# Moving the causal mask of the SSD branch from the exponent to the score block, and the log decays from GpSimd to VectorE

## The chip, the core and the metric

The kernel runs on one core of a Trainium2 chip. The metric is device time in microseconds (us), the median of several executions; lower is better. TensorE (PE) does the matrix products, VectorE (DVE), ScalarE (ACT) and GpSimd (POOL) the elementwise work, each from a queue of its own in program order. SyncE (SP) issues the weight loads; ACT issues some DMAs from its own queue.

## The reference

One decoder layer over 256 tokens of width 2048. A combined projection feeds stick-breaking attention, a Mamba-2 SSD branch and memory cross-attention; each branch is projected back, weighted by sigmoid gates and summed, and an output projection, a residual and a final norm follow. The part that the change touches is the SSD scan, 32 heads of 64 channels in 8 groups:

```python
a_cum = jnp.cumsum(a_dt, axis=-1)                       # dt * a, never positive
tri = jnp.tril(jnp.ones((l, l), dtype=bool))
seg = a_cum[..., :, None] - a_cum[..., None, :]
decay_in = jnp.exp(jnp.where(tri, seg, -jnp.inf))       # 0 for sources later than the target
cb = jnp.einsum('bclgn,bcsgn->bcgls', cm, bm)           # scores, one block per group
y_diag = jnp.einsum('bcgls,bgecls,bcsgep->bclgep', cb, decay_in, xs)
```

A head's weight from source token s to target token t is thus the score times exp of the difference of two running sums where s <= t, and 0 elsewhere.

## The kernel before

**Weight products.** Nearly all time goes to products of the 256 tokens with weight matrices. `gemm` makes 512 columns at a time. It walks the contraction in chunks of two tiles of 128: SP loads a chunk of 512 KB (`raw`), ACT rounds it to a high part (`wh`, L139), DVE forms the remainder (`wl`, L143), and PE does twelve products of 512 columns (L230 high x high, L231 with `wl`, L232). `wh` and `wl` have three buffers each, so that PE reads one chunk while the next two are made: ACT can begin chunk n when PE has left chunk n - 3.

**Order by hand.** The instructions of each engine run as they are traced. After each chunk `pump` traces what was put off until now (`defer`) and one step of one of two lanes of background work, in turn; a lane so advances every second chunk. A step is what a generator does up to its next `yield`.

**The background work around the change.** `ssd_group(g)` is one group of four heads; groups 0, 2, 4, 6 stand in one lane, 1, 3, 5, 7 in the other. It runs beside the gate products and the projections of the memory and stick-breaking branches: four pairs of eight and four chunks for either branch, 96 chunks in all. The lanes get their first SSD step at the eighth of them. Before the third branch the lanes are emptied (`finish()`). The steps of a group:

1. PE transposes the group's x (`xp`, L656). ACT issues two DMAs that spread rows of `acT`, the running sums by head, over all partitions: two tiles `dec`, each of two heads by two halves of the tokens, 128x512 (L661).
2. ACT copies `xp` to `xn` (L666). POOL adds the mask `dmask` (0 or -1e30) to each `dec` (L674) and then the source's running sum `nac`, once for each half (L677): six instructions. Behind them POOL makes `xs`, `xn` and `xe` (L681 to L684), five instructions. PE makes the scores `cb` (L687, L688).
3. ACT copies the score block between the halves (L690) and takes Exp of both `dec` (L692).
4. DVE multiplies both `dec` by `cb`, which it reads from PSUM (L695).
5. PE applies them to `xs` (`y`, L702) and makes `off` (L704).
6. to 8. DVE adds the parts and gates them (L706 to L711), ACT and POOL make the group norm (L714, L132, L133), and ACT scales (L719).

`ssd_cols` afterwards turns the eight results round (`dot`, L732), two steps for each group.

Of the kernel before, what the change touches and what calls it, by code (L numbers as in the profile page):

```python
# [16 lines left out]
P = 128  # L17
D = 2048          # model width
T = 256           # tokens, and memory tokens
NKT = D // P  # L20
GW = 512          # columns of a weight group
KC = 2            # k-tiles per weight chunk
# [18 lines left out]
def trunk_kernel(  # L41
# [35 lines left out]
    def tq(shape, n):  # L77
        return tmp.tile(shape, F32, tag="tq", name=nm(n), bufs=2)
# [3 lines left out]

    def bank(shape, n="bank"):
        return psB.tile(shape, F32, tag="bank", name=nm(n))
# [15 lines left out]
    # keeps the array busy, so that its clock is up when the first operands arrive  # L100
# [8 lines left out]
    tri = const.tile([P, P], F32, name="tri")          # [s, t] = 1 where s <= t  # L109
    nc.gpsimd.affine_select(out=tri, in_=ones, compare_op=ALU.is_ge, fill=0.0,  # L110
                            base=0, pattern=[[1, P]], channel_multiplier=-1)
    smask = const.tile([P, P], F32, name="smask")      # 0 where k < q, else NEG
    dmask = const.tile([P, P], F32, name="dmask")      # 0 where s <= t, else NEG
    nc.gpsimd.memset(dmask, 0.0)
    for m, op in ((smask, ALU.is_gt), (dmask, ALU.is_ge)):
        nc.gpsimd.affine_select(out=m, in_=dmask, compare_op=op, fill=NEG, base=0,
                                pattern=[[1, P]], channel_multiplier=-1)
# [17 lines left out]
    def split(*parts):  # L135
        """hi + lo = src * scale for each (hi, lo, src, scale), hi and lo in the form of
        float32r."""
        for hi, _, src, scale in parts:
            nc.scalar.activation(hi, src, AF.Copy, **({} if scale is None else {"scale": scale}))  # L139
        for hi, lo, src, scale in parts:  # L140
            h32 = hi.bitcast(F32)
            if scale is None:
                nc.vector.tensor_tensor(lo, src, h32, ALU.subtract)  # L143
            else:
                nc.vector.scalar_tensor_tensor(lo, src, scale, h32, ALU.mult, ALU.subtract)

    class Cols:
        """A [K, 256] operand by k-tiles, in slots of 8 k-tiles, as hi and lo."""
# [12 lines left out]
    def defer(fn, chunks=LATE):  # L161
        """Has fn traced that many weight chunks later."""
        cnt[0] += 1
        heapq.heappush(late, (now[0] + chunks, cnt[0], fn))
# [9 lines left out]
    def pump():  # L174
        """Once per weight chunk: what was put off until now, and one step of a lane of the
        work that runs beside the weight products."""
        now[0] += 1
        while late and late[0][0] <= now[0]:
            heapq.heappop(late)[2]()
        advance(lanes[now[0] % 2])  # L180
# [19 lines left out]
    def gemm(lhs, nk, w, c0, evac, cols=False, along=None, sizes=None):  # L200
        """evac gets lhs @ w[:, c0:c0 + 512], in two banks: by halves of the tokens, or
        with cols transposed, by pairs of blocks of 128 columns."""
        acc = [psA.tile([P, GW], F32, tag="acc", name=nm("acc")) for _ in range(2)]
        k0 = 0
        for kc in sizes or [KC] * (nk // KC):
            raw = load_chunk(w, c0, GW, k0, kc)
            wh = stage.tile([P, kc, GW], F32R, tag="wh", name=nm("wh"))
            wl = stage.tile([P, kc, GW], F32R, tag="wl", name=nm("wl"))
            split((wh, wl, raw, None))
            if along is not None:  # L210
                along(k0)
            for j in range(kc):
                kt = k0 + j
                lh, ll = lhs.at(kt)
                first, last = kt == 0, kt == nk - 1
                if cols:
                    for b in range(4):
                        a = acc[b // 2][:, (b % 2) * T:(b % 2 + 1) * T]
                        bs = slice(b * P, (b + 1) * P)
                        nc.tensor.matmul(a, wh[:, j, bs], lh, start=first and b % 2 == 0,  # L220
                                         stop=False, skip_group_check=True)
                        nc.tensor.matmul(a, wh[:, j, bs], ll, start=False, stop=False,  # L222
                                         skip_group_check=True)
                        nc.tensor.matmul(a, wl[:, j, bs], lh, start=False, stop=last,  # L224
                                         skip_group_check=True)
                    continue
                for t in range(2):
                    a = acc[t]
                    tt = slice(t * P, (t + 1) * P)
                    nc.tensor.matmul(a, lh[:, tt], wh[:, j], start=first, stop=False)  # L230
                    nc.tensor.matmul(a, lh[:, tt], wl[:, j], start=False, stop=False)  # L231
                    nc.tensor.matmul(a, ll[:, tt], wh[:, j], start=False, stop=last)  # L232
            k0 += kc
            pump()
        if cols:
            acc = [a.rearrange("p (b t) -> p b t", t=T) for a in acc]
        defer(lambda: evac(acc))

    def to_cols(dst, b0, scale):
        """Evacuates a transposed group into blocks dst[:, b0 + i, token]."""  # L240
# [43 lines left out]
    def squares(raw, acc, q, first=None):  # L284
        """Adds the squares of 4 k-tiles to acc, by tokens."""
# [12 lines left out]
    def scale_steps(rs, rbc, acc):  # L298
        """1 / rms of the 256 tokens, on the tokens' own partitions and then on every one."""
# [64 lines left out]
    # the gains and the first k-tile in one  # L364
# [18 lines left out]
    acT = dram.tile([SSD_HEADS, T], F32, name="acT")  # L383

    def dt_steps():
        """The step sizes' projection, transposed: the 32 columns' high and low parts side by
        side as the stationary operand, then one sum over both."""
# [26 lines left out]
        # log1p(e) = 2 atanh(e / (2 + e)), e in [0, 1]  # L414
# [17 lines left out]
        # nac = - cumulative sum of dt * a in each half = cumulative sum of dt * exp(a_log)  # L432
# [6 lines left out]
        # decays to the end of the first half, and from there  # L439
# [104 lines left out]
    oS = Cols(8, "oS")  # L544
    ra = const.tile([P, P], F32R, name="ra")           # 1 where s > t
    rb = const.tile([P, P], F32R, name="rb")           # 1

    def sb_head(h):
        hs = slice(h * P, (h + 1) * P)
        # blocks (k, q) of 128 by 128: (0, 0), (1, 1), (0, 1)  # L550
# [22 lines left out]
        # the last block of the second product goes unused: it makes 256 columns  # L573
# [23 lines left out]
    def start_sb():  # L597
        nc.gpsimd.tensor_tensor(tri, ones, tri, ALU.subtract)     # now 1 where s > t
# [50 lines left out]
    def ssd_group(g):  # L649
# [18 lines left out]
        xe = tq([P, 3, P], "xe")       # 256 of xs at the edge, 128 of cb  # L668
# [3 lines left out]
        for i, d in enumerate(dec):  # L672
            d4 = d.rearrange("p h q t -> p (h q) t")
            nc.gpsimd.tensor_tensor(d4, d4, dmask.unsqueeze(1).to_broadcast([P, 4, P]), ALU.add)  # L674
            for q in range(2):
                h2 = slice(4 * g + 2 * i, 4 * g + 2 * i + 2)
                nc.gpsimd.tensor_tensor(d[:, :, q], d[:, :, q],  # L677
                                        nac[:, q, h2].unsqueeze(2).to_broadcast([P, 2, P]),
                                        ALU.add)
# [10 lines left out]
        nc.scalar.activation(xe[:, 2], cb[:, 1], AF.Copy)  # L690
        for d in dec:
            nc.scalar.activation(d, d, AF.Exp)  # L692
        yield
        for d in dec:
            nc.vector.tensor_tensor(d, d, cb[:, 0:3:2].unsqueeze(1).to_broadcast([P, 2, 2, P]),  # L695
                                    ALU.mult)
# [157 lines left out]
    # the last group half by half, so that one half's end hides under the other  # L854
# [30 lines left out]
def lay_out(inputs):  # L885
    """Every array without its leading 1; x, mem and the vectors by channels also or only
    channel-major, [channel % 128, channel // 128, ...]."""
# [29 lines left out]
```

## Time and profile before

| what | value |
|---|---|
| time, median of 3 executions | 1259.33 us (1258.82 to 1260.66) |
| profiled execution, span of the core | 1256.4 us |
| PE busy | 1239.0 us (99%) |
| DVE busy | 760.4 us (61%) |
| ACT busy | 596.6 us (47%) |
| POOL busy | 172.9 us (14%) |

No other time of the profiled execution is given than its span; the median stands 2.9 us above it. The profile records start and duration of each instruction. Where an engine waits, a row names the time and the instruction that ended it. Matmuls overlap: their ends are modelled, and the next one starts before the one in front has ended.

### The profile page before, as it was taken

What the parts mean: (1) busy time and instruction counts of PE and PEld (TensorE: products, weight loads), DVE (VectorE), ACT (ScalarE), POOL (GpSimd) and SP (SyncE); (2) the same over time, 40 slices, a digit from 0 to 9 for tenths busy, and PEclk for the clock granted to TensorE, in tenths of its full rate; (3) what the DMA queues carried; (4) which work ended last, traced back from release to release, by engine and by line L of the source; (5) the groups of instructions that cost most, each with busy time, mean ns of one, the idle gap of its engine ahead of it and who ended that gap; (6) DMA issues with size and microseconds to landing.
All of it is one profiled execution on the core that took longest, in us unless ns stands there. A gap on an engine that the chain in (4) does not pass through costs nothing.

```text
span 1256.4 us, 18790 instructions
## 1 busy us (share of the span) xinstructions
PE 1239.0 (99%) x7512; PEld 1109.7 (88%) x7512; DVE 760.4 (61%) x925; ACT 596.6 (47%) x734; POOL 172.9 (14%) x178
## 2 busy tenths in 40 slices
PE   9999999999999999999999999999999999999997
PEld 7899999999988889999999787877888888888886
DVE  7765554555544545788888765564665555555554
ACT  6653433443444554434554554555444444444443
POOL 3500000000000000010100616436111110110101
PEclk9999999999999999999999999999999999999999
DMA  8666566654566666565666666646566676667573
GB/s 300 223 203 176 160 188 176 183 166 142 163 194 193 184 169 185 169 179 169 172 173 199 190 184 202 209 145 193 181 179 199 201 203 199 184 193 246 198 240 120
DMA packets 124681, 236.57 MB, mean 188 GB/s; under 512 B 10128, under 2 KB 11568, under 8 KB 124464
## 3 DMA queue, kind: packets, MB, share of 16 engines
q1 hardware_dynamic: 118272, 224.01, 60.0%
q10 hardware_dynamic: 6320, 11.35, 2.7%
q8 instruction: 59, 0.97, 0.3%
q14 instruction: 30, 0.25, 0.1%
HBM read 233.20 MB, written 2.13 MB: 187 GB/s over the span
## 4 chain that ended last, share of the span: by engine, by line
PE 88%; POOL 5%; DMA 2%; DVE 2%; issue 1%; ACT 1%; POOLq 0%; SPq 0%; ACTq 0%; DVEq 0%
PE acc L231 15%; PE acc L232 15%; PE acc L230 15%; PE acc L220 12%; PE acc L222 12%; PE acc L224 12%; POOL dec L677 2%; POOL dec L674 2%; DMA raw<-in_w_mem_kv_dram 1%; PE y L702 1%; DMA dec<-acT 1%; DVE wl L143 1%; POOL xn L683 1%; PE acc L873 1%; PE acc L874 1%
## 5 line engine op out<-in xcount | busy, mean ns | idle before, releaser
L143 DVE TENSOR_TENSOR wl<-raw,wh 128x1024 fp32r<-128x1024 f32 (+1 forms) x410 | 514.0, 1256 | 390.5 <-ACT wh L139 388.9
L139 ACT ACTIVATE wh<-raw 128x1024 fp32r<-128x1024 f32 (+1 forms) x410 | 430.9, 1054 | 514.2 <-PE acc L232 271.9
L220 PE MATMUL acc<-hTh,wh 128*128 128x256 f32 x1152 | 327.4, 284 | 0.0
L222 PE MATMUL acc<-hTl,wh 128*128 128x256 f32 x1152 | 325.9, 283 | 0.0
L224 PE MATMUL acc<-hTh,wl 128*128 128x256 f32 x1152 | 325.9, 283 | 0.0
L231 PE MATMUL acc<-wl,hTh 128*128 128x512 f32 x576 | 225.0, 391 | 3.8 <-DVE wl L143 3.7
L230 PE MATMUL acc<-wh,hTh 128*128 128x512 f32 x576 | 227.9, 396 | 0.7 <-ACT wh L139 0.7
L232 PE MATMUL acc<-wh,hTl 128*128 128x512 f32 x576 | 224.5, 390 | 0.0
L222 PEld LDWEIGHTS acc<-hTl,wh 128*128 128x128 f32 x1152 | 221.1, 192 | 0.0
L220 PEld LDWEIGHTS acc<-hTh,wh 128*128 128x128 f32 x1152 | 221.0, 192 | 0.1
L224 PEld LDWEIGHTS acc<-hTh,wl 128*128 128x128 f32 x1152 | 221.0, 192 | 0.0
L231 PEld LDWEIGHTS acc<-wl,hTh 128*128 128x128 f32 x576 | 108.3, 188 | 27.5 <-DVE wl L143 6.1
L230 PEld LDWEIGHTS acc<-wh,hTh 128*128 128x128 f32 x576 | 108.2, 188 | 23.4 <-ACT wh L139 1.9
L232 PEld LDWEIGHTS acc<-wh,hTl 128*128 128x128 f32 x576 | 108.1, 188 | 22.7
L567 POOL TENSOR_TENSOR lm<-lm,sp 128x384 f32<-128x384 f32 x8 | 11.4, 1430 | 402.3 <-DVE sp L566 402.3
L776 POOL TENSOR_TENSOR merged<-merged,sig 128x512 f32<-128x512 f32 x16 | 27.4, 1735 | 242.7 <-DVE sig L775 242.7
L632 DVE SCALAR_TENSOR_TENSOR cT<-cu,wcols,cT 128x255 f32<-128x255 f32 (+2 forms) x96 | 47.9, 499 | 3.4
L230 PE MATMUL acc<-wh,oDh 128*128 128x512 f32 x128 | 49.8, 389 | 0.0
L231 PE MATMUL acc<-wl,oDh 128*128 128x512 f32 x128 | 49.8, 389 | 0.0
L232 PE MATMUL acc<-wh,oDl 128*128 128x512 f32 x128 | 49.8, 389 | 0.0
L674 POOL TENSOR_TENSOR dec<-dec,dmask 128x512 f32<-128x512 f32 x16 | 23.9, 1493 | 131.0 <-PE acc L232 108.9
L230 PE MATMUL acc<-wh,mTh 128*128 128x512 f32 x96 | 37.4, 390 | 0.0
(256 smaller groups left out, 1509.4 us busy)
## 6 DMA issues: line engine op xcount, KB each, us to landing
raw<-in_w_in_dram SPq DMA_DIRECT2D x288, 512.0 KB, 3.8
raw<-in_w_branch_ssd_dram SPq DMA_DIRECT2D x32, 512.0 KB, 4.2
raw<-in_w_out_dram SPq DMA_DIRECT2D x32, 512.0 KB, 4.7
raw<-in_w_mem_kv_dram SPq DMA_DIRECT2D x30, 512.0 KB, 4.7
raw<-in_w_branch_mem_dram SPq DMA_DIRECT2D x16, 512.0 KB, 4.1
raw<-in_w_branch_sb_dram SPq DMA_DIRECT2D x16, 512.0 KB, 4.2
dec<-acT ACTq DMA_DIRECT2D x16, 256.0 KB, 6.4
sig<-in_b_gate_dram ACTq DMA_DIRECT2D x12, 256.0 KB, 4.4
```

Source lines behind the costliest of these rows:

```text
L139: nc.scalar.activation(hi, src, AF.Copy, **({} if scale is None else {"scale": scale}))
L143: nc.vector.tensor_tensor(lo, src, h32, ALU.subtract)
L220: nc.tensor.matmul(a, wh[:, j, bs], lh, start=first and b % 2 == 0, stop=False, skip_group_check=True)
L222: nc.tensor.matmul(a, wh[:, j, bs], ll, start=False, stop=False, skip_group_check=True)
L224: nc.tensor.matmul(a, wl[:, j, bs], lh, start=False, stop=last, skip_group_check=True)
L230: nc.tensor.matmul(a, lh[:, tt], wh[:, j], start=first, stop=False)
L231: nc.tensor.matmul(a, lh[:, tt], wl[:, j], start=False, stop=False)
L232: nc.tensor.matmul(a, ll[:, tt], wh[:, j], start=False, stop=last)
L632: nc.vector.scalar_tensor_tensor(a[:, s:T], u[:, 0:T - s], convw[:, 3 - s, i:i + 1], a[:, s:T], ALU.mult, ALU.add)
L674: nc.gpsimd.tensor_tensor(d4, d4, dmask.unsqueeze(1).to_broadcast([P, 4, P]), ALU.add)
L677: nc.gpsimd.tensor_tensor(d[:, :, q], d[:, :, q], nac[:, q, h2].unsqueeze(2).to_broadcast([P, 2, P]), ALU.add)
L776: nc.gpsimd.tensor_tensor(merged[t][:, cs], merged[t][:, cs], sig[:, t], ALU.add)
```

## The change

The mask no longer goes into the exponent. A constant `past` of ones and zeros replaces `dmask`. `ssd_group` loses POOL's six instructions on `dec`; in a step of its own, between steps 2 and 3, DVE makes min(dec + nac, 0) with eight instructions on 128x128, one for each head and half. Where s <= t the difference is not positive and the clip does nothing; elsewhere it keeps Exp at 1 or less. Then DVE multiplies the two diagonal score blocks by `past` into a tile `cbm`, which takes the buffers of the tag `cu`, and both `dec` are multiplied by `cbm`, in SBUF, instead of `cb`, in PSUM. ACT's copy of the score block between the halves moves from the step of Exp to the step of the product. A group has nine steps instead of eight. Comments go, too.

```diff
+    def small2(shape, n):
+        return tmp.tile(shape, F32, tag="cu", name=nm(n), bufs=2)
...
-    dmask = const.tile([P, P], F32, name="dmask")      # 0 where s <= t, else NEG
-    nc.gpsimd.memset(dmask, 0.0)
-    for m, op in ((smask, ALU.is_gt), (dmask, ALU.is_ge)):
-        nc.gpsimd.affine_select(out=m, in_=dmask, compare_op=op, fill=NEG, base=0,
-                                pattern=[[1, P]], channel_multiplier=-1)
+    past = const.tile([P, P], F32, name="past")
+    nc.gpsimd.memset(past, 0.0)
+    nc.gpsimd.affine_select(out=smask, in_=past, compare_op=ALU.is_gt, fill=NEG, base=0,
+                            pattern=[[1, P]], channel_multiplier=-1)
+    nc.gpsimd.affine_select(out=past, in_=ones, compare_op=ALU.is_ge, fill=0.0, base=0,
+                            pattern=[[1, P]], channel_multiplier=-1)
...
-        for i, d in enumerate(dec):
-            d4 = d.rearrange("p h q t -> p (h q) t")
-            nc.gpsimd.tensor_tensor(d4, d4, dmask.unsqueeze(1).to_broadcast([P, 4, P]), ALU.add)
-            for q in range(2):
-                h2 = slice(4 * g + 2 * i, 4 * g + 2 * i + 2)
-                nc.gpsimd.tensor_tensor(d[:, :, q], d[:, :, q],
-                                        nac[:, q, h2].unsqueeze(2).to_broadcast([P, 2, P]),
-                                        ALU.add)
...
         yield
-        nc.scalar.activation(xe[:, 2], cb[:, 1], AF.Copy)
+
+        for i, d in enumerate(dec):
+            for e in range(2):
+                for q in range(2):
+                    h = 4 * g + 2 * i + e
+                    nc.vector.tensor_scalar(d[:, e, q], d[:, e, q], nac[:, q, h:h + 1], 0.0,
+                                            ALU.add, ALU.min)
+        yield
         for d in dec:
             nc.scalar.activation(d, d, AF.Exp)
         yield
+        nc.scalar.activation(xe[:, 2], cb[:, 1], AF.Copy)
+        cbm = small2([P, 2, P], "cbm")
+        nc.vector.tensor_tensor(cbm, cb[:, 0:3:2], past.unsqueeze(1).to_broadcast([P, 2, P]),
+                                ALU.mult)
         for d in dec:
-            nc.vector.tensor_tensor(d, d, cb[:, 0:3:2].unsqueeze(1).to_broadcast([P, 2, 2, P]),
+            nc.vector.tensor_tensor(d, d, cbm.unsqueeze(1).to_broadcast([P, 2, 2, P]),
                                     ALU.mult)
```

## Rows read from the trace of the kernel before

**Rows 1.** The page of the profile: busy time of each engine over the span.

```profile
PE 1239.0 (99%) x7512; PEld 1109.7 (88%) x7512; DVE 760.4 (61%) x925; ACT 596.6 (47%) x734; POOL 172.9 (14%) x178
```

**Rows 2.** Busy time of each engine in stretches of 50 us, with instruction counts, the granted share of PE's clock, the DMA share and GB/s: the stretch before the SSD steps and four with them. The last row is the sum over these four.

```profile
640.00:690.00 50.00, 50.00 (x381) 48.34 (x381) 40.60 (x63) 23.92 (x23) 0.00 (x0) 1.00 0.68 194
690.00:740.00 50.00, 48.71 (x234) 39.90 (x233) 36.28 (x46) 24.48 (x32) 21.65 (x24) 1.00 0.60 183
740.00:790.00 50.00, 49.01 (x237) 40.66 (x236) 28.91 (x35) 28.18 (x40) 21.57 (x25) 1.00 0.64 195
790.00:840.00 50.00, 48.24 (x232) 39.68 (x230) 29.04 (x32) 26.40 (x37) 23.12 (x26) 1.00 0.62 189
840.00:890.00 50.00, 47.71 (x224) 39.03 (x224) 28.50 (x32) 24.43 (x37) 24.84 (x28) 1.00 0.64 192
sum 200.00, PE 193.66 PEld 159.26 DVE 122.73 ACT 103.51 POOL 91.18; mean PE 48.42 PEld 39.82 DVE 30.68 ACT 25.88 POOL 22.80
```

**Rows 3.** Who waited for whom, PE alone, from 690 to 905 us: us in total, times, longest us.

```profile
PE acc L231 <- DVE wl L143: 4.9, 7, 0.9
PE acc L230 <- ACT wh L139: 1.3, 3, 0.6
```

**Rows 4.** PE's instructions in order of time (start us, duration us) around one of these waits.

```profile
718.77 0.49 PE L230 MATMUL acc<-wh,hTh 128*128 128x512 f32 x1
720.07 0.50 PE L231 MATMUL acc<-wl,hTh 128*128 128x512 f32 x1 [0.81 <-DVE wl L143]
```

**Rows 5.** The chain of work that ended last, from 711 to 726 us (start us, us, what).

```profile
711.22 1.24 POOL dec L674
...
715.06 2.06 POOL dec L677 x2
...
717.67 1.05 ACT wh L139
...
724.74 1.15 DVE wl L143
...
725.93 0.50 PE acc L231
```

**Rows 6.** Groups of instructions by line, 690 to 905 us: count, busy us, mean ns of one, idle time of the engine in front and what ended it.

```profile
L677 POOL TENSOR_TENSOR dec<-dec,nac 128x256 f32<-128x256 f32 x32 | 26.4, 844 | 1.3
L674 POOL TENSOR_TENSOR dec<-dec,dmask 128x512 f32<-128x512 f32 x16 | 23.9, 1493 | 131.0 <-PE acc L232 108.9 <-DMA dec<-acT 22.1
L692 ACT ACTIVATE dec<-dec 128x512 f32<-128x512 f32 x16 | 9.7, 628 | 11.9 <-POOL dec L677 11.8
L695 DVE TENSOR_TENSOR dec<-dec,cb 128x512 f32<-128x512 f32 x16 | 10.2, 675 | 0.0
```

**Rows 7.** Groups of DVE instructions by line and shape over the whole span, the columns of rows 6.

```profile
L627 DVE TENSOR_TENSOR cu<-acc,rbc_x 128x256 f32<-128x256 f32 x32 | 13.4, 417 | 0.0
L143 DVE TENSOR_TENSOR oMl<-mo,oMh 128x512 fp32r<-128x512 f32 x4 | 2.8, 692 | 2.8 <-ACT oMh L139 2.8
L422 DVE TENSOR_SCALAR dtw<-dtw 128x64 f32<-128x64 f32 x8 | 1.6, 195 | 0.3
L311 DVE TENSOR_SCALAR dg<-ident,rs_x 128x128 f32<-128x128 f32 x2 | 0.5, 283 | 0.0
L629 DVE TENSOR_SCALAR cT<-cu,wcols 128x256 f32<-128x256 f32 x32 | 14.8, 464 | 1.2
```

**Rows 8.** One undisturbed chunk on ACT, DVE and PE (start us, duration us): its high part, its remainder, PE's first product two chunks ahead of it, and PE's first product of the chunk itself.

```profile
796.10 1.06 ACT L139 ACTIVATE wh<-raw 128x1024 fp32r<-128x1024 f32 x1 [0.81 <-PE acc L232]
797.20 1.23 DVE L143 TENSOR_TENSOR wl<-raw,wh 128x1024 fp32r<-128x1024 f32 x1 [1.45 <-ACT wh L139]
795.90 0.39 PE L230 MATMUL acc<-wh,hTh 128*128 128x512 f32 x1
801.34 0.39 PE L230 MATMUL acc<-wh,hTh 128*128 128x512 f32 x1
```

**Rows 9.** The instructions on the tile `dec`: time of its DMAs from issue to landing.

```profile
DMA to landing us min/median/max: 4.2/6.4/8.6
```

**Rows 10.** DVE and POOL in order of time where they meet (start us, duration us).

```profile
699.61 1.52 DVE L629 TENSOR_SCALAR cT<-cu,wcols 128x256 f32<-128x256 f32 x1
699.68 1.30 POOL L674 TENSOR_TENSOR dec<-dec,dmask 128x512 f32<-128x512 f32 x1 [98.51 <-PE acc L232]
706.13 0.61 POOL L681 TENSOR_TENSOR xs<-xn,dts 128x256 f32<-128x256 f32 x1
706.70 1.23 DVE L143 TENSOR_TENSOR wl<-raw,wh 128x1024 fp32r<-128x1024 f32 x1 [1.00 <-ACT wh L139]
706.82 1.58 POOL L683 TENSOR_TENSOR xn<-xn,drow 128x256 f32<-128x256 f32 x1
714.09 1.97 DVE L143 TENSOR_TENSOR wl<-raw,wh 128x1024 fp32r<-128x1024 f32 x1 [3.35 <-ACT wh L139]
```

**Rows 11.** PE in order of time at the borders of the SSD work: the first gate product, the first transposes of a group, the last transposes of `ssd_cols`, and the first gate product of the third branch.

```profile
680.37 0.40 PE L230 MATMUL acc<-wh,hTh 128*128 128x512 f32 x1
702.16 0.60 PE L656 MATMUL xp<-ident,cT 128*128 128x128 f32 x4
952.05 0.60 PE L732 MATMUL dot<-ident,zD 128*128 128x128 f32 x4
982.42 0.39 PE L230 MATMUL acc<-wh,hTh 128*128 128x512 f32 x1
```

## The prediction, made before the changed kernel was run

> **What bounds the kernel now.** I read the page first. PE is busy for 1239.0 of 1256.4 us, POOL for 172.9 [rows 1]: work taken off POOL can pay only where PE waits for it. So the second view is the busy time by stretches. In the 50 us ahead of the SSD steps PE has no gap; in the four stretches with SSD steps it is busy for 193.66 of 200 us, 6.3 us short, at a granted clock of 1.00 throughout, and POOL, idle before, is busy for 22 to 25 us of each [rows 2]. The third view, the waits, names them: ten waits of PE for the weight split, 4.9 us for the remainder `wl` and 1.3 us for the high part `wh` [rows 3]. These 6.2 us are not yet what PE loses, since the ends of matmuls are modelled. In the undisturbed stretch PE begins a chunk at 795.90 and the one two further at 801.34 [rows 8]: 24 products in 5.44 us, one every 0.227 us, though each is shown with 0.39. A wait thus hides 0.39 - 0.227 = 0.16 us in the last matmul's modelled end. Where PE starts L230 at 718.77 and the next at 720.07, 1.30 us passed instead of 0.23, so 1.07 were lost; the row shows 0.81 [rows 4], 0.26 less. Ten waits hide between 1.6 and 2.6 us. **PE loses 7.8 to 8.8 us beside the SSD work; I take 8.0**, the nearer end, since most waits follow a matmul shown with 0.39.
>
> The Trainium skill warns of this ("Perfetto Trace Analysis", Identifying the Most-Contended Engine: matmul busy time says little on the distance to the limit, because matmuls are pipelined). By PE's busy share alone the loss would be 6.3 us; by the starts it is larger, and I go by the starts.
>
> The last view is the chain, which tells why the split is late [rows 5]. POOL works through the second group's `dec` (L674, L677) until 717.1; ACT, in program order, can't take Exp of it sooner, and the `wh` behind Exp starts at 717.67; DVE's products and its `wl` follow, and the last of the late `wl` lets PE go on at 725.93. Over the whole stage ACT's Exp waited 11.8 us for L677 [rows 6]. POOL is not short of time on average; what hurts is that both lanes hand it a group one chunk apart and ACT's queue blocks on the second.
>
> **What the change removes.** From POOL, per group, two L674 of 1.493 and four L677 of 0.844 us: 6.4 us, 50.3 us in all [rows 6], and above all ACT's wait for them. Five POOL instructions stay (`xs`, `xn`, `xe`), which are read only at step `y`, six or more chunks later.
>
> **What it adds to DVE.** The trace has no add-and-minimum on 128x128. Its nearest row is a TENSOR_SCALAR on 128x128 with a scalar per partition, 0.283 us; a smaller one (128x64) takes 0.195, a two-operation one on 128x256 takes 0.464 [rows 7]. I take 0.283, by shape: 8 x 0.283 = 2.3 us per group, bounds 1.6 and 3.7. `cbm`, from PSUM on 128x256, is like L627: 0.417. The two products now read SBUF twice: 0.692 (the 128x512 remainder) for 0.675 [rows 7, 6], so nothing. Together 2.7 us per group, 21.5 us over eight (bounds 16 and 33), while DVE has 200 - 123 = 77 us idle in these stretches [rows 2].
>
> **Whether DVE's bursts reach PE.** DVE's queue also holds the `wl`. In the undisturbed chunk `wl` ends at 797.20 + 1.23 = 798.43 and PE starts that chunk at 801.34, needing `wl` one product later, 801.57 [rows 8]: 3.1 us of slack. A chunk takes PE 2.72 us. The adds of the two lanes fall into consecutive chunks: 1.23 + 2.3 = 3.5 us each, 0.8 us too much, 1.6 us late after both. With the products: 1.23 + 0.417 + 1.38 = 3.0, late by 0.3 each; a gate evacuation of two 512-column instructions (some 1.4 us by the 0.692 row) that falls between the two makes it 2.0. Both are below 3.1, and the chunks behind them, with 1.5 us to spare each, make it good. At the upper bound the adds are 4.9 us a chunk, 4.4 us late after both, 1.3 us of stall per pair, 5 us over four pairs. That end stays in the range.
>
> **The new waits.** The adds wait for the DMA of `dec`. It is issued in step 1, the adds stand in step 3: four chunks or 10.9 us later, and the longest landing took 8.6 [rows 9]. Should one be late, the `wl` behind the adds wait too and then PE; before, POOL alone waited. With the slack of 3.1 us a landing under 14 us costs nothing. Exp stands two chunks behind the adds and the products two behind Exp; each finds its operand done. ACT's copy of the score block (0.26 us) moves to another chunk and waits for nothing: nothing. Number and queues of the DMAs stay, and so does PE's work.
>
> **The ninth step.** Each lane has four groups, then four `ssd_cols` of two steps: 40 steps before, 44 after, every second chunk. The first stands at the eighth chunk of 96; the last transposes now run at 952.05 and the third branch starts at 982.42 [rows 11], eleven chunks later. Four more steps are eight chunks: they still end before `finish()` and cost nothing. Without that room each step left over would run without products beside it. Constants: as many POOL instructions as before. `cbm` takes the `cu` buffers after the convolution is done with them.
>
> **Sum.** The waits go, no new one is left: 1256.4 - 8.0 = 1248.4 us of span; the median stands 2.9 above the profiled span: **1251.3 us**. With the loss at 8.8 it is 1250.5.
>
> **The port.** DVE and POOL hold each other up: L629 began at 699.61, L674 at 699.68, and L629 lasted until L674 was done, 1.52 us instead of its mean of 0.46; POOL's 128x256 instruction took 0.61 alone and 1.58 beside a `wl` [rows 10, 7]. By the Trainium skill ("SBUF — State Buffer", Who interferes with whom) a DVE instruction with two SBUF inputs, or one that uses both ports as TENSOR_SCALAR can, contends with GpSimd for a port pair that one of them holds for its whole instruction. The trace agrees. That speaks against the change: the adds are TENSOR_SCALAR, and the products, which with `cb` in PSUM had one SBUF input, get two. In numbers: POOL's ten instructions that stay for a pair of groups take 0.61 each when alone. If DVE meets every one of them in the two chunks of the adds and waits it out, that is 6.1 us, late by 1.6 + 6.1 = 7.7, beyond the slack by 4.6: over four pairs 18 us lost, 8.0 saved.
>
> **The rivals.**
> - *A. The waits vanish:* 1250.5 to 1252.3. For it: DVE's room and ACT's 11.8 us. 0.68.
> - *B. DVE's bursts keep part of them:* with adds near their upper bound, or some of POOL's instructions in the way, about half comes back, 1255.3. For it: late `wl` already show as PE's releaser. Against: DVE's longest burst today, `wl` 1.97 us and products behind it, was late because ACT held it up first. 0.14.
> - *C. The change doesn't do what it says:* the waits come from ACT's own burst (Exp beside the sigmoid) or the DVE backlog, and stay: 1259. Against: the chain passes through POOL for each pair, and Exp itself takes only 1.3 us per group. 0.10.
> - *D. Slower, by the port:* POOL's ten instructions per pair stand in front of the adds as worked out above: 1259.3 - 8.0 + 18 = 1269. It decides against the change once DVE's waits for POOL exceed 3.1 - 1.6 + 2.0 = 3.5 us per pair. For it: the row of L629. Against: with 22 POOL instructions per pair today, the `wl` beside them grew from 1.23 to at most 1.97; POOL's part shrinks by half, and its five run mostly a step ahead of the adds. 0.08.
>
> **How the numbers follow.** A measurement of this kernel can tell about 0.2% (2.5 us) from no change. Faster: A and nearly all of B, 0.82; the same: C, 0.10; slower: D, 0.08. The range begins at 1250.0, half a microsecond below the larger loss for the spread of the runs, and reaches to 1256.0 through B; C and D, 0.18, are left out.
>
> **What would show it.** In the profile after: the four stretches with PE full; no row in which ACT's Exp waits for POOL; POOL down by about 50 us, DVE up by about 21; eight adds per group of some 0.28 us; the last `dot` some 22 us later but ahead of the third branch. PE's waits for `wl` right behind adds that last 0.8 us or more would show B or D; waits of the adds for the DMA would show that the four chunks don't suffice; Exp or `wh` late with POOL done would show C.

## The result, and the profile after

The changed kernel takes 1249.29 us (median of 4 executions, 1248.51 to 1249.70) against 1259.84 us for the kernel before (4 executions). The ratio is 0.992 with a 95% interval of 0.9908 to 0.9932: faster, by 10.5 us. The direction was the forecast one; the time lies 2.0 us below the forecast value and 0.7 us below the range. The profiled execution took 1249.63 us with a span of 1247.6 us, 8.8 us less than the span before.

The page, busy time of each engine, to be held against [rows 1]:

```profile
PE 1234.8 (99%) x7512; PEld 1108.9 (89%) x7512; DVE 775.9 (62%) x997; ACT 596.3 (48%) x734; POOL 123.2 (10%) x130
```

POOL lost 49.7 us (forecast: about 50). DVE gained 15.5 net, less than the forecast 21, though the additions themselves came to 22.4 (below): its other work became shorter, for instance the weight splits (L143 before, L147 now), 514.0 us before and 510.1 after by the page.

Busy time by stretches, the columns of [rows 2]:

```profile
640.00:690.00 50.00, 50.00 (x386) 48.53 (x385) 40.56 (x63) 22.92 (x23) 0.00 (x0) 1.00 0.65 193
690.00:740.00 50.00, 50.00 (x245) 42.10 (x243) 38.52 (x61) 26.72 (x33) 7.86 (x11) 1.00 0.63 198
740.00:790.00 50.00, 50.00 (x235) 41.65 (x234) 35.27 (x50) 29.49 (x38) 9.82 (x14) 1.00 0.65 209
790.00:840.00 50.00, 50.00 (x238) 41.83 (x238) 36.04 (x54) 25.50 (x38) 9.83 (x14) 1.00 0.62 196
840.00:890.00 50.00, 50.00 (x244) 42.07 (x243) 32.90 (x48) 26.45 (x39) 13.33 (x16) 1.00 0.60 194
```

PE is full in all four stretches with SSD steps, where it lacked 6.3 us by modelled ends before. The ten waits of [rows 3] have no row left.

ACT's waits from 690 to 985 us (who waited for whom, us in total, times, longest us):

```profile
ACT wh L143 <- PE acc L236: 89.4, 53, 3.9
ACT wh L143 <- issue: 16.2, 7, 3.2
ACT oDh L143 <- PE dot L739: 14.0, 8, 2.1
```

Before, Exp waited 11.8 us for POOL [rows 6]. No such row is left; most of what ACT waits for is PE, which is as it should be in a kernel that PE bounds.

The added DVE work, 690 to 912 us, in the columns of [rows 6], and then the two bursts of adds of the first pair, in order of time:

```profile
L691 DVE TENSOR_SCALAR dec<-dec,nac 128x128 f32<-128x128 f32 x64 | 19.1, 366 | 0.0
L702 DVE TENSOR_TENSOR dec<-dec,cbm 128x512 f32<-128x512 f32 x16 | 10.3, 688 | 0.3
L699 DVE TENSOR_TENSOR cbm<-cb,past 128x256 f32<-128x256 f32 x8 | 3.3, 417 | 0.0
```

```profile
710.36 3.11 DVE L691 TENSOR_SCALAR dec<-dec,nac 128x128 f32<-128x128 f32 x8
713.39 1.21 DVE L147 TENSOR_TENSOR wl<-raw,wh 128x1024 fp32r<-128x1024 f32 x1
714.53 1.65 DVE L691 TENSOR_SCALAR dec<-dec,nac 128x128 f32<-128x128 f32 x8
716.10 1.21 DVE L147 TENSOR_TENSOR wl<-raw,wh 128x1024 fp32r<-128x1024 f32 x1
```

Eight adds take 1.65 us alone (by the records they overlap a little) and 3.11 where POOL works beside them. `cbm` and the products came out at the durations taken from [rows 7].

**The stage on PE.** The cleanest measure is from the first transposes of the SSD work to the first product of the third branch's projection, which holds the same work in every variant. Before, it ran from 702.16 [rows 11] to this product:

```profile
1004.18 0.39 PE L230 MATMUL acc<-wh,oDh 128*128 128x512 f32 x1
```

and after, from and to:

```profile
703.34 0.60 PE L660 MATMUL xp<-ident,cT 128*128 128x128 f32 x4
...
965.28 0.60 PE L739 MATMUL dot<-ident,zD 128*128 128x128 f32 x4
...
973.90 0.39 PE L234 MATMUL acc<-wh,hTh 128*128 128x512 f32 x1
...
995.66 0.39 PE L234 MATMUL acc<-wh,oDh 128*128 128x512 f32 x1
```

That is 302.02 us before and 292.32 after: 9.7 us gained. The span shows only 8.8, mostly since the first transposes came 1.2 us later in this execution, before any changed instruction on that path; behind the stage the rest of the kernel took 0.3 us less. The last `dot` stands 8.6 us ahead of the third branch (965.28 to 973.90): the ninth step did find its room.

### The profile page after: what moved, and what is told of

It is laid out like the page before. It is cut to its first block, busy times and chain, and to the rows that moved or that the text cites. A ratio compares the mean times of both kernels' runs of the same rounds, so it can differ in the third digit from the quotient of the medians.

```text
span 1247.6 us, 18787 instructions
## 1 busy us (share of the span) xinstructions
PE 1234.8 (99%) x7512; PEld 1108.9 (89%) x7512; DVE 775.9 (62%) x997; ACT 596.3 (48%) x734; POOL 123.2 (10%) x130
## 4 chain that ended last, share of the span: by engine, by line
PE 94%; DMA 2%; ACT 1%; DVE 1%; issue 1%; POOL 0%; SPq 0%; POOLq 0%; ACTq 0%; DVEq 0%
PE acc L234 17%; PE acc L236 17%; PE acc L235 17%; PE acc L224 12%; PE acc L228 12%; PE acc L226 12%; DMA raw<-in_w_mem_kv_dram 2%; PE y L709 1%; DVE wl L147 1%; PE acc L881 1%; PE acc L879 1%; PE acc L880 1%; ACT wh L143 0%; PE off L711 0%; PE dtp L401 0%
## 5 line engine op out<-in xcount | busy, mean ns | idle before, releaser
L147 DVE TENSOR_TENSOR wl<-raw,wh 128x1024 fp32r<-128x1024 f32 (+1 forms) x410 | 510.1, 1245 | 365.6 <-ACT wh L143 364.2
L143 ACT ACTIVATE wh<-raw 128x1024 fp32r<-128x1024 f32 (+1 forms) x410 | 431.9, 1054 | 523.5 <-PE acc L236 265.5
L236 PE MATMUL acc<-wh,mTl 128*128 128x512 f32 x96 | 37.4, 389 | 0.0
```

## The experiments

**The two kernels again.** The kernel before against itself:

> The kernel before against itself, to see how the time of an execution stands to its span and how much both spread. Theory 'size' (the forecast only mis-sized PE's loss and the distance between span and time): time about 1259.8 us, span 1256.4 to 1257.4, the distance 2.0 to 2.9 us. Rival 'unlike profile' (the one profiled execution of before was a quick one): spans of 1257.5 us and more in the other executions.

1260.04 us (11 executions, 1258.58 to 1260.83), ratio to the kernel before 0.9996 (0.9987 to 1.0005). Over the 32 executions of the kernel before in this comparison the span went from 1255.7 to 1260.0 us, median 1258.3, and the time stood 1.7 us above it. The profiled execution on which the prediction rests, 1256.4, was near the quick end. The rival "unlike profile" thus came true, and theory "size" had both the spans and the distance wrong. The profile of this run, PE in order of time around the first pair's waits, and the stretch's window (columns of [rows 2]):

```profile
718.55 0.39 PE L232 MATMUL acc<-wh,hTl 128*128 128x512 f32 x1
719.86 0.50 PE L230 MATMUL acc<-wh,hTh 128*128 128x512 f32 x1 [0.93 <-ACT wh L139]
721.17 0.50 PE L231 MATMUL acc<-wl,hTh 128*128 128x512 f32 x1 [0.80 <-DVE wl L143]
721.50 0.40 PE L232 MATMUL acc<-wh,hTl 128*128 128x512 f32 x1
...
722.00 0.63 PE L231 MATMUL acc<-wl,hTh 128*128 128x512 f32 x1
722.43 0.63 PE L232 MATMUL acc<-wh,hTl 128*128 128x512 f32 x1
722.86 0.63 PE L230 MATMUL acc<-wh,hTh 128*128 128x512 f32 x1
```

```profile
720.00:725.00 5.00, 4.20 (x12) 3.07 (x13) 5.00 (x7) 1.71 (x2) 2.08 (x3) 0.69 0.53 116
```

Two things stand here that the forecast lacked. The product behind a wait is followed by the next only after 0.33 us (721.17 to 721.50), not 0.227. And behind two waits close together the granted clock fell: in this stretch its mean is 0.69, and eight products follow each other at some 0.43 us, the pace of 1.2 GHz, instead of 0.227, which costs 8 x 0.2 = 1.6 us. That is most of the 2.0 us between the spans of the two profiles. In the profile shown before, the same stretch had a clock of 1.00 [rows 2].

The changed kernel again:

> The changed kernel again. Theory 'size': PE loses no wait any more, gain of 9 to 10 us, time 1249 to 1250.5 us, distance of time and span as for the kernel before. Rival 'luck of the runs': the gain falls back to the 8.0 us of the forecast, time 1251.3 us or more.

1249.18 us (1248.97 to 1249.32), ratio 0.9911 (0.9898 to 0.9925). The gain is 10.9 us; theory "size" holds for the time, but not for the distance between time and span, which was 2.1 us here and 1.7 for the kernel before. Eight executions of the changed kernel have spans from 1246.5 to 1247.6, a range of 1.1 us, where the 32 of the kernel before had 4.3. Taken as standard deviations, which allow for the different numbers, that is 0.4 against 1.0 us.

**The step alone.**

```diff
         nc.tensor.matmul(cb[:, 2], bT[:, g, P:T], cTT[:, g, P:T], start=True, stop=True)
         yield
+        yield
         nc.scalar.activation(xe[:, 2], cb[:, 1], AF.Copy)
         for d in dec:
             nc.scalar.activation(d, d, AF.Exp)
```

> The kernel before with nothing but the additional step between the mask adds on GpSimd and Exp. Theory 'ACT's queue' (what cost time was Exp standing in ACT's queue before GpSimd had finished): the longest wait of Exp for GpSimd was 2.9 us, a step is 5.4 us, so the waits vanish with all of GpSimd's work still there: 1249.5 to 1251 us. Rival 'work and port' (the gain comes from taking 50 us of work off GpSimd, which holds VectorE up): 1257 to 1260 us.

1250.22 us, ratio 0.992 (0.9906 to 0.9933). POOL does all that it did, and the kernel before with one empty `yield` is within 1.0 us of the changed kernel. The rival "work and port" falls. PE's and ACT's waits, 690 us on:

```profile
PE acc L231 <- DVE wl L143: 0.8, 2, 0.4
```

```profile
ACT dec L693 <- POOL dec L677: 7.2, 4, 1.9
```

Exp still waits for POOL four times, but two waits of PE are left, 0.8 us; the remaining difference to the changed kernel is theirs. In the stage it is 1.4 us (702.85 to 996.54, 293.69 against 292.32); by the starts, the two waits and the products behind them cost just that.

**The change without the step.**

```diff
                     nc.vector.tensor_scalar(d[:, e, q], d[:, e, q], nac[:, q, h:h + 1], 0.0,
                                             ALU.add, ALU.min)
-        yield
         for d in dec:
             nc.scalar.activation(d, d, AF.Exp)
```

> The changed kernel without the step of its own: the eight adds stand directly ahead of Exp in one step. Theory 'ACT's queue': Exp waits for the adds, which stand behind the weight split on VectorE (1.2 us and then 1.7 to 3.1 us), for both groups of a pair one chunk apart; late by about 6 us after both, 3 us beyond the slack of 3.1, four pairs: some 8 to 14 us lost against the changed kernel, 1257 to 1263 us. Rival 'work and port': GpSimd's work is gone all the same, 1249 to 1251 us.

1261.92 us, ratio 1.0016 (1.0007 to 1.0024), against 1249.2 with the step: 12.7 us lost, and the gain with it, inside the 1257 to 1263 expected. Its waits:

```profile
PE acc L235 <- DVE wl L147: 7.6, 7, 2.4
PE acc L234 <- ACT wh L143: 0.7, 4, 0.2
```

```profile
ACT dec L694 <- DVE dec L691: 16.8, 14, 2.3
```

Exp now waits for DVE's adds, 16.8 us instead of the 11.8 for POOL. POOL's freed 50 us buy nothing.

**The adds on POOL, with the step.**

```diff
-                    nc.vector.tensor_scalar(d[:, e, q], d[:, e, q], nac[:, q, h:h + 1], 0.0,
+                    nc.gpsimd.tensor_scalar(d[:, e, q], d[:, e, q], nac[:, q, h:h + 1], 0.0,
```

> The changed kernel with its eight adds per group on GpSimd instead of VectorE. By GpSimd's row of 0.61 us for 128x256 with two inputs I estimate 0.35 us each, 2.8 us per group, with the five others 5.9 us per group. Theory 'ACT's queue': a pair then keeps GpSimd for some 12 us, Exp stands two chunks behind, nobody waits: 1249 to 1250.5 us, like the changed kernel. Rival 'engine' (VectorE is what makes it fast): 1253 to 1260 us, with waits of Exp for GpSimd.

1272.98 us, ratio 1.0102 (1.0086 to 1.0118): a miss for both theories. My price was wrong. One such instruction takes POOL 0.71 us and more:

```profile
L691 POOL TENSOR_SCALAR dec<-dec,nac 128x128 f32<-128x128 f32 x64 | 50.0, 799 | 0.0
```

so POOL keeps all the time that the change had taken off it. It also makes the adds a step later than in the step-alone kernel, one step ahead of Exp instead of two:

```profile
ACT dec L695 <- POOL dec L691: 26.1, 14, 2.1
```

That is the same mechanism at a higher price: 26.1 us of Exp waiting. PE's waits, 690 to 1000 us:

```profile
PE acc L234 <- ACT wh L143: 8.6, 4, 2.2
PE acc L235 <- DVE wl L147: 4.8, 8, 0.8
```

Besides these 13.4 us, the granted clock had a mean of 0.94 to 0.99 in four of the six stretches of 50 us from 690 us on, about 6.5 us more. Two things follow. This kernel has nine steps too, so the number of steps is not what saves the time. And in the step-alone kernel POOL was busy on `dec` for longer still (55.8 us: 30.2 in L677, 25.6 in L674), yet PE waited for only 0.8 us. What counts is how many steps lie between the work on `dec` and Exp against how long that work takes, and not the engine as such.

**The old mask, on DVE.** The constant `dmask` takes the place of `past` again, and `cbm` goes.

```diff
...
-                    nc.vector.tensor_scalar(d[:, e, q], d[:, e, q], nac[:, q, h:h + 1], 0.0,
-                                            ALU.add, ALU.min)
+                    nc.vector.scalar_tensor_tensor(d[:, e, q], d[:, e, q], nac[:, q, h:h + 1],
+                                                   dmask, ALU.add, ALU.add)
...
-            nc.vector.tensor_tensor(d, d, cbm.unsqueeze(1).to_broadcast([P, 2, 2, P]),
+            nc.vector.tensor_tensor(d, d, cb[:, 0:3:2].unsqueeze(1).to_broadcast([P, 2, 2, P]),
```

> The changed kernel with the mask back in the exponent: eight instructions of VectorE add the running sum and the mask of 0 or -1e30 at once, and the products read the score block from PSUM; no masked copy of the block. Theory 'ACT's queue': where the mask is applied costs nothing, 1249 to 1250.5 us. Rival 'mask' (the move of the mask itself saves time): some microseconds above the changed kernel.

1248.72 us, ratio 0.9913 (0.9898 to 0.9929), executions from 1248.59 to 1249.81: the same as the changed kernel within the spread of either, and the stage takes 292.32 us (703.76 to 996.08) to the hundredth. Where the mask is applied is worth nothing.

**DVE's room.** One and two more passes of adds, which leave the values as they are:

```diff
                     nc.vector.tensor_scalar(d[:, e, q], d[:, e, q], nac[:, q, h:h + 1], 0.0,
                                             ALU.add, ALU.min)
+                    nc.vector.tensor_scalar(d[:, e, q], d[:, e, q], 0.0, 0.0,
+                                            ALU.add, ALU.min)
```

> The changed kernel with a second, idempotent pass of eight adds of zero per group. It measures VectorE's room. By the forecast's slack of 3.1 us: a chunk with the adds then takes VectorE 1.2 + 3.3 us, and 1.4 us more where GpSimd holds it up in the first; late by 3.2 after the first and 5.0 after the second, 1.9 beyond the slack, four pairs: 1256 to 1258 us. Rival 'more room' (the weight split runs further ahead than I worked out): 1249 to 1251 us.

1257.56 us, ratio 0.9985 (0.9976 to 0.9994), inside the 1256 to 1258 worked out from the slack of 3.1 us. PE waits once per pair, right behind the adds:

```profile
PE acc L235 <- DVE wl L147: 7.0, 4, 1.8
```

> The same with two additional passes: 1.2 + 4.9 us in each of the two chunks, late by 4.8 and 8.2, 5.1 beyond the slack of 3.1, four pairs: about 1269 us, with PE waiting for the weight split right behind the adds. Rival 'more room': below 1258 us.

1284.48 us, ratio 1.0192 (1.0176 to 1.0209), against 1269 expected. The waits grew as worked out, 21.5 us against 5.1 x 4 = 20:

```profile
PE acc L235 <- DVE wl L147: 21.5, 8, 3.9
```

The rest is the clock (columns of [rows 2]):

```profile
690.00:740.00 50.00, 44.20 (x194) 35.93 (x193) 41.73 (x86) 23.48 (x27) 7.76 (x10) 0.97 0.59 184
740.00:790.00 50.00, 45.81 (x215) 37.72 (x214) 35.45 (x76) 24.88 (x36) 9.77 (x14) 0.96 0.47 155
790.00:840.00 50.00, 50.00 (x237) 41.91 (x236) 33.01 (x43) 23.41 (x33) 9.77 (x14) 0.97 0.68 207
840.00:890.00 50.00, 44.19 (x200) 36.36 (x199) 36.30 (x77) 23.49 (x35) 1.99 (x4) 0.93 0.47 145
890.00:940.00 50.00, 44.25 (x205) 36.42 (x204) 37.36 (x78) 22.04 (x28) 11.36 (x13) 0.93 0.51 164
```

Of each 50 us the shares 0.03, 0.04, 0.03, 0.07 and 0.07 are missing, 12 us in all. By this rough count waits and clock make 33.5 us; the kernel is 35 slower than the changed one.

**One step too many.** An empty tenth step behind the adds:

```diff
                                             ALU.add, ALU.min)
         yield
+        yield
```

> The changed kernel with one more empty step, ten for a group. It tests the forecast's sentence that the ninth step is free only because there is room ahead of the third branch: a lane then needs 48 steps and gets 44 or 45 ahead of the emptying of the lanes. Theory 'room': three or four steps of each lane, transposes and splits of the last groups, are left over and run without products beside them; four groups' splits hold ACT and VectorE for some 4 us in front of the next weight chunk, of which the buffers hide about 3: 1250 to 1253 us, PE with a gap between 970 and 1000 us. Rival 'steps are free': 1249.2 us, like the changed kernel.

1254.36 us, ratio 0.9962 (0.9948 to 0.9975), 5.1 us above the changed kernel and 1.4 above the range expected. What is left over when the lanes are emptied stands in front of the third branch:

```profile
971.78 1.91 PE L740 MATMUL dot<-ident,zD 128*128 128x128 f32 x16
976.44 0.80 PE L234 MATMUL acc<-wh,hTh 128*128 128x512 f32 x1 [2.75 <-ACT wh L143]
977.71 0.80 PE L235 MATMUL acc<-wl,hTh 128*128 128x512 f32 x1 [0.47 <-DVE wl L147]
```

Sixteen transposes in a row, then 2.75 and 0.47 us of waiting; and the doubled durations of these two rows are again the clock, which I had not counted:

```profile
976.00:983.00 7.00, 6.09 (x14) 4.44 (x15) 5.12 (x7) 2.48 (x4) 2.33 (x2) 0.53 0.59 183
```

A mean of 0.53 over 7 us costs 3.3 us, so waits and clock weigh the same here. This profiled execution was the slowest of the five (1256.03 us).

## Why the prediction was wrong, point by point

- **What bounds the kernel, and the chain: right.** PE's waits beside the SSD work were the whole reserve, and they came from Exp standing in ACT's queue before its operand was ready. The step-alone kernel shows it best: POOL's work untouched, and 9.8 us gone.
- **PE's loss of 8.0 us: the step that failed, mis-sized.** It measured 9.7 us in the same profile's stage (302.02 to 292.32). The starts of all of PE's products in that stage of the kernel before give it piece by piece. Eleven gaps, one of them (0.10 us, at 725.93) too short for [rows 3], cost 8.56 us by the starts; that lies inside my bounds of 7.8 to 8.8, of which I took the nearer end. I left out what comes behind a wait. The two products that follow the wait of [rows 4] at 720.07:

```profile
720.41 0.40 PE L232 MATMUL acc<-wh,hTl 128*128 128x512 f32 x1
720.64 0.40 PE L230 MATMUL acc<-wh,hTh 128*128 128x512 f32 x1
```

The first comes after 0.34 us instead of 0.227. That happens behind eight of the gaps (behind the other three the next product waits again), 0.88 us in all, and the ten products after each of these lose another 0.26 us in all: 8.56 + 0.88 + 0.26 = 9.70. With 9.7 in place of 8.0 the forecast would have been 1249.6, below my range already.

- **The median 2.9 us above the profiled span: the other step that failed.** I took this distance for a constant. It is 1.7 to 1.9 us in every execution of the kernel before that lists both, and up to 2.3 in the other kernels. The rest was that the profiled execution was quick, 1256.4 against a median span of 1258.3. In the one execution profiled again, 1.6 of the 2.0 us more were the fall of the granted clock behind the waits. Of the others only the mean clock is known: of the 32, the eight with 0.995 or less had a mean span of 1259.1 us, the eight with 0.998 had 1257.2. That fits, but it does not show that all of the excess belongs to the waits.
- **How the two make 2.0 us.** The span was forecast at 1248.4 and came out at 1247.6, 0.8 less: 1.7 us more gained in the stage, less the 1.2 us by which the stage began later, plus the 0.3 us gained behind it. The other 1.2 us are the distance from this span to the median, 1.7 us instead of 2.9.
- **What is added to DVE: right.** 0.283 was taken and 0.366 measured as a mean, 0.274 as a median, the difference being the adds that met POOL; 22.4 us in all against 21.5. The slack of 3.1 us and the 2.72 us of a chunk gave the doubled adds to within the range.
- **The new waits: right.** No add waited for the DMA of `dec`, and Exp and products found their operands.
- **The ninth step: right, and dearer to miss than I expected.** It fits by three chunks; one step more costs 5.1 us. But I costed the step at nothing and looked for the gain in POOL's time. The last `dot` came 13.2 us later and not 22, since the waits in front of it are gone. The runs show the opposite weight: the step carries the gain, and the move to DVE alone, without it, is slower than the kernel before (1261.92).
- **The rivals.** A came true in its mechanism, at a time below its 1250.5 to 1252.3. B did not come true, DVE kept its slack. C was wrong, the waits went; but none of the four says what the runs showed, that relieving POOL is not what saved the time. D, the port: the first burst of a pair did stretch from 1.65 to 3.11 us where POOL ran beside it, 1.5 us in each of the four pairs instead of the 6.1 of the worst case, below the 3.5 from which it would have decided. The longest `wl` beside POOL's work on `dec` was 2.03 us (at 805.36), not the 1.97 that I named for B and D; it changes neither.
- **The lower bound.** I set the range half a microsecond under the larger loss for the spread of the runs, as if that spread were noise that stays. The standard deviation of the spans is 0.7 to 1.1 us in the kernels whose PE waits for 3 us or more, and 0.3 to 0.5 in the changed kernel, the step alone and the old mask: the spread went with the waits, so part of it is what the change removes.

What is not settled: why the clock falls behind some of these waits and not behind others. Length alone does not tell: it fell behind 0.93 and 0.80 us in the kernel before, and did not behind 2.16 and 0.76 us, again with one product between them, in the adds on POOL (from 728.12 on, with the products behind at 0.227 us). No run here was made to tell.

## What to carry to other kernels

When an in-order engine shows a wait for another engine's result, try first to trace the consumer one step later; here one empty `yield` gave nine tenths of the gain (9.8 of 10.9 us), and moving the work without it gave nothing. Count whether the schedule has room for the step. Measure what a wait costs by the starts of the work around it up to where the steady pace returns, and look whether the spread between executions goes with the waits, as it did here.

## What the runs showed of the hardware

- After two waits of PE, 0.93 and 0.80 us with one product between them, the granted clock fell to 1.2 GHz: eight products at some 0.43 us instead of 0.227. In another execution of the same kernel it did not fall at this place, and in the adds on POOL it did not fall behind waits of 2.16 and 0.76 us.
- Behind a wait of PE the next product began 0.33 to 0.34 us after the one that had waited, instead of 0.227 us (in the kernel before, eight times).
- A POOL TENSOR_SCALAR with a scalar per partition took 0.71 us for 128x128 (median 0.711, least 0.707), longer than a two-input POOL instruction on twice as much, 0.61 us for 128x256 [rows 10].
- A DVE TENSOR_SCALAR on 128x128 took 0.27 us and up to 0.65 where POOL worked beside it.
